# A fused two-block layer on one Trainium2 core: how the first expert layer leaves PSUM, and how its expert lists are made

## The chip, the cores and the metric

The kernel runs on one core of one Trainium2 chip. The metric is device time in microseconds (us), the median of three runs; lower is better.

## The reference

256 tokens of width 2048 pass through a first block (sliding-window attention beside a short convolution, then a gate) and a second block (a linear recurrence beside attention over selected keys, then a layer of many small experts). The change lies in that last layer, which in the reference reads:

```python
q = (xf @ wq).reshape(t, PEER_HEADS, PEER_QDIM)
...
top_s, pos = lax.top_k(cand_s, PEER_TOPK)
expert = jnp.take_along_axis(cand_i, pos, axis=-1).reshape(t, -1)
gate = jax.nn.softmax(top_s.astype(jnp.float32), axis=-1).astype(x.dtype).reshape(t, -1)
...
z = jnp.einsum('cd,ced->ce', xc, u[ec])
act = jax.nn.gelu(z, approximate=False) * gc
return jnp.einsum('ce,ced->cd', act, v[ec])
```

There are 128 x 128 = 16384 experts; each token takes 16 of them for each of 8 heads, so 128 in all.

## The kernel before

All products with weights run through one stream of weight tiles, 128 x 2048 float32 of 1 MB each (`stream`, L387). A tile is loaded into one of three `raw` buffers by SP, cut in two halves of 1024 columns, and each half is split into a high part `whi` by ACT (L415, five buffers) and a low part `wlo` by DVE (L422, four buffers), three halves ahead of the half that PE is at. One turn of the loop at L437 is one half: `cut_hi` for the half three ahead, `self.step()`, `cut_lo` for that half, the matmuls of this half, and after the last half of a pair of tiles whatever leaves PSUM. The instructions of each engine run in the order in which this loop writes them, so an instruction that waits holds all that stand behind it on its engine.

`step()` (L346) hands out the side work: it goes over the first three tasks in a list and lets each run to its next `yield`; the numbers yielded are charged against a credit for each half (1.3 in this layer, overdrafts carried over), and 0 costs nothing but a turn.

The expert layer (`peer`, L1237) streams, in this order:

- 16 tiles of `w_pq` (queries of the heads), then
- 128 tiles of `peer_u`, numbered 0 to 127 here. Together they hold every expert's first vector; the hidden products of all 16384 experts are computed and stored. From tile 24 on a half is 8 matmuls of 512 columns (L467) and 8 of 256 (L468), until then three of 256 each. After each pair of tiles `post_u` (L1577) takes it out of its PSUM buffer `mm` (two buffers of a pair): ACT copies one part (L336), DVE adds the other and multiplies by the row scale (L339, L340), ACT applies Gelu and starts the store to the table `zg` in HBM (L1581, L1582);
- one tile and then 107 rows of experts gathered from `peer_v`, by lists of the experts in use.

Beside the first two, the side work finds which experts are in use:

- `head_task` (L1291) finds the top 16 of a head on DVE and then has POOL scatter the gates into the table: 16 indirect DMAs for each half of 128 tokens (`scatter`, L1356). Scatters of the same half of two heads wait for each other, as both add into the same column of the table. Heads 0 to 2 (`EARLY` = 3) scatter both halves, heads 3 to 7 the first half alone; the second halves of heads 3 to 7 follow at the end, in `gates_task` (L1371). They are 256 indirect DMAs in all.
- `mask_task` (L1417) runs once for each half of the tokens, from the tile in `U_MASK` on. It reads the half's gates back in 8 chunks of 1 MB (SP, L1426, into four `vraw` buffers) behind the half's last scatter, and DVE takes the maximum over tokens (L1444). For the second half POOL first adds one half of the chunk to the other (L1437).
- `list_task` (L1456) turns the masks into lists of experts in 37 pieces of up to three columns of a list. A piece is: POOL compares (L1503), DVE makes the 0/1 matrix `hot` (L1510), PE multiplies it (three matmuls, L1520) into a PSUM bank, ACT takes two results from the bank (L1528, L1529), DVE sums (L1535). The banks are the two of `bg1`. Piece i's products are written in one step, its ACT part in the next, its sum in the one after.
- `row_source` (L1627) loads an expert row through the lists. It is called seven tiles ahead, by `load` (L400) from `cut_lo`, and runs `step()` until the lists are there, however many steps that takes, before the stream goes on.

```python
                    if i + RAW_BUFS + ROW_BUFS < n and callable(items[i + RAW_BUFS + ROW_BUFS][0]):
                        load(i + RAW_BUFS + ROW_BUFS)
```

Of the kernel before, what the change touches and what calls it, by code (L numbers as in the profile page):

```python
# [17 lines left out]
P = 128  # L18
# [36 lines left out]
DUMMY = P * P  # L55
U_MERGE = 24
LAST = 3
U_MASK = (63, 96)
EARLY = 3
ROWS = 7  # L60
COEF = 6

# [184 lines left out]
class Build:  # L247
# [139 lines left out]
    def stream(self, items):  # L387


        n = len(items)  # L390
        raw, cut, order = {}, {}, []
        fills = {FILL_FROM + FILL_STEP * j: j for j in range(FILLS)}
        while len(order) < 2 * n:
            i = len(order) // 2
            if items[i][1].crossed:
                order += [(i, 0), (i + 1, 0), (i, 1), (i + 1, 1)]
            else:
                order += [(i, 0), (i, 1)]

        def load(i, a=0, b=2 * HALF):  # L400
            if i < n and callable(items[i][0]):
                raw[i] = items[i][0]()
                return
            if i < n:
                if a == 0:
                    raw[i] = self.strm.tile([P, 2 * HALF], F32, name="raw", tag="raw", bufs=RAW_BUFS)
                self.nc.sync.dma_start(raw[i][:, a:b], items[i][0][:, a:b])
                if i in fills and b == 2 * HALF:
                    self.fill(fills.pop(i))

        def cut_hi(k):
            if k < 2 * n:
                i, half = order[k]
                hi = self.strm.tile([P, HALF], F32R, name="whi", tag="whi", bufs=CUT_BUFS)
                self.S.activation(hi, raw[i][:, half * HALF:(half + 1) * HALF], AF.Copy)  # L415
                cut[k] = [hi, None]

        def cut_lo(k):
            if k < 2 * n:
                i, half = order[k]  # L420
                lo = self.strm.tile([P, HALF], F32R, name="wlo", tag="wlo", bufs=CUT_BUFS - 1)
                self.V.tensor_tensor(lo, raw[i][:, half * HALF:(half + 1) * HALF], cut[k][0].bitcast(F32),  # L422
                                     op=ALU.subtract)
                cut[k][1] = lo
                if half:
                    del raw[i]
                    if i + RAW_BUFS < n and not callable(items[i + RAW_BUFS][0]):
                        load(i + RAW_BUFS)
                    if i + RAW_BUFS + ROW_BUFS < n and callable(items[i + RAW_BUFS + ROW_BUFS][0]):
                        load(i + RAW_BUFS + ROW_BUFS)  # L430

        self.prologue(load)
        for k in range(AHEAD):
            cut_hi(k)
            cut_lo(k)
            self.prologue_step(k)
        for k, (i, half) in enumerate(order):  # L437
            self.pos = i
            cut_hi(k + AHEAD)
            self.step()  # L440
            cut_lo(k + AHEAD)
            hi, lo = cut.pop(k)
            items[i][1](half, hi, lo)
            if half and items[i][2]:
                items[i][2]()
# [791 lines left out]
    def peer(self):  # L1237
# [144 lines left out]
        def begin_lists():  # L1382
            t = self.actp.tile([P, 2 * KC * TOK], F32, name="lists", tag=f"act{free}")
            at = [0]

            def cut(*dims, dt=F32):
                size = int(np.prod(dims))
                v = t[:, at[0]:at[0] + size]
                at[0] += size + size % 2
                if dt is not F32:  # L1390
                    v = v.bitcast(dt)
                if len(dims) > 1:
                    ax = " ".join("abcd"[:len(dims)])
                    v = v.rearrange(f"p ({ax}) -> p {ax}", **dict(zip("abcd", dims)))
                return v

            offsets, n = CONST_AT["consts3"]
            c3 = cut(n)
            self.nc.sync.dma_start(c3, A["consts3"])
            for name, (o, w) in offsets.items():  # L1400
                self.cons[name] = c3[:, o:o + w]
            st["abs"], st["gt"] = cut(2, PIECE * P), cut(2, PIECE, P)
            st["hot"], st["prer"] = self.t([2, PIECE * P], "hot", dt=F32R), self.t([PIECE, 3, 130], "pre", dt=F32R)
            st["scratch"] = t[:, 0:at[0]]
            st["m"], st["cls"], st["pre"] = cut(2, P), cut(3, P), cut(3, 132)
            st["n"], st["mid"], st["half"], st["end"] = (cut(3) for _ in range(4))
            st["bias"], st["high"] = cut(40), cut(40)
            st["sum"], st["row"], st["rho"] = cut(NLIST), cut(NLIST), cut(NLIST)
            st["zat"], st["vat"], st["over"] = cut(NLIST, dt=U32), cut(NLIST, dt=U32), cut(2, dt=mybir.dt.int32)
            st["zg"], st["gates"], st["cd"] = cut(ROWS, 2, TOK), cut(TOK), [None, None]  # L1410
            assert at[0] <= 2 * KC * TOK
# [5 lines left out]
        def mask_task(ti):  # L1417
            while self.pos < u0 + U_MASK[ti]:
                yield 0.0
            chunks = {}  # L1420

            def load(g):
                if g < 8:
                    gt = self.t([2 * HALF], "vraw", ROW_BUFS)
                    gv = chunks[g] = gt.rearrange("p (b t) -> p b t", b=16)
                    d = self.nc.sync.dma_start(gv, table[:, 16 * g:16 * g + 16, 1, ti * P:(ti + 1) * P])  # L1426
                    for other in scatters[1 - ti] if ti == 0 else ():
                        self.tc.declare_no_dep(d.ins, other.ins, reason="gates of other tokens")
                    behind(d, scatters[ti][-1])

            for g in range(3):
                load(g)
                yield 0.0
            def half(g):
                if ti and g < 8:
                    chunk, chunks[g] = chunks[g], chunks[g][:, :, 0:P // 2]
                    G.tensor_tensor(chunks[g], chunks[g], chunk[:, :, P // 2:P], op=ALU.add)  # L1437

            half(0)
            yield 0.0  # L1440
            for g in range(8):
                load(g + 3)
                half(g + 1)
                V.tensor_reduce(st["m"][:, ti, 16 * g:16 * g + 16], chunks[g], axis=AX.X, op=ALU.max)  # L1444
                yield 1.25 if ti else 2.3
            V.tensor_scalar(st["m"][:, ti], st["m"][:, ti], 0.0, None, op0=ALU.is_gt)
            V.memset(st["m"][:, ti, P - 1:P], 0.0)
            if ti:
                d = self.nc.sync.dma_start(st["gates"], table[:, P - 1, 1])
                for k in range(2):  # L1450
                    behind(d, scatters[k][-1])
            yield 0.2
            if ti:
                yield from list_task()

        def list_task():  # L1456
# [32 lines left out]
            for c in range(3):  # L1489
# [3 lines left out]
                    V.tensor_scalar(out[:, o:o + n], self.con("starts", o, o + n), -1.0, edge[:, c:c + 1],  # L1493
                                    op0=ALU.mult, op1=ALU.add)
                o += n
            yield 1.4

            def late(i):

# [10 lines left out]
                    V.scalar_tensor_tensor(st["hot"][:, i % 2, :n * P], self.con("slots", 0, n * P), hi[:, k:k + 1],  # L1510
                                           st["abs"][:, i % 2, :n * P], op0=ALU.is_le, op1=ALU.mult)

            banks = {}

            def products_of(i):
                if i < len(pieces):
                    c, b, n = pieces[i]
                    ps = self.bg1()
                    for j in range(n):
                        T.matmul(ps[:, 130 * j:130 * j + 130], st["hot"][:, i % 2, j * P:(j + 1) * P],  # L1520
                                 st["prer"][:, j, c], start=True, stop=True)
# [2 lines left out]
            def signs(i):  # L1524
                if 0 <= i < len(pieces):
                    c, b, n = pieces[i]
                    col, pv = CLASS_AT[c] + b, banks.pop(i)
                    S.activation(st["row"][:, col:col + n], pv[:, 0:n, P], AF.Copy)  # L1528
                    S.activation(st["gt"][:, i % 2, 0:n], pv[:, 0:n, 0:P], AF.Sign, bias=self.con("past", col, col + 1))  # L1529

            def sums(i):
                if i >= 0:
                    c, b, n = pieces[i]
                    col = CLASS_AT[c] + b
                    V.tensor_reduce(st["sum"][:, col:col + n], st["gt"][:, i % 2, 0:n], axis=AX.X, op=ALU.add)  # L1535

            late(0)
            late(1)
            yield 0.0
            yield 0.0  # L1540
            hot(0)
            yield 0.0
            for i in range(len(pieces) + 2):
                late(i + 2)
                hot(i + 1)
                sums(i - 2)
                signs(i - 1)
                products_of(i)
                yield 1.25
            rho = st["rho"]  # L1550
# [25 lines left out]

        def post_u(i):  # L1577
            def f(ps):
                z = self.t([2, TOK], "z", 3)
                self.scaled(z, ps)  # L1580
                S.activation(z, z, AF.Gelu)  # L1581
                d = self.nc.scalar.dma_start(table[:, i:i + 2, 0], z)  # L1582
                for other in scatters[0] + scatters[1]:
                    self.tc.declare_no_dep(d.ins, other.ins, reason="gates stand beside the hidden products")
                stores.append(d)
            return f

        def post_last(j):

            def f(ps):  # L1590
                if j == 0:
                    st["zlast"] = self.t([2, TOK], "z", 3)
                z = st["zlast"][:, j]
                S.activation(z, ps[:, j, 1], AF.Copy)
                V.tensor_tensor(z, z, ps[:, j, 0], op=ALU.add)
# [205 lines left out]
```

## Time and profile before

| | |
|---|---|
| median of three runs | 2518.39 us (2518.31 to 2519.71) |
| the profiled execution | 2519.8 us, of which 2518.0 us are its span |
| PE busy | 2454.8 us, 97% of the span |
| DVE, ACT, POOL busy | 1793.1, 1347.5, 815.8 us |
| mean granted TensorE clock | 0.992 of full speed |
| HBM | 218 GB/s over the span |

The profile follows one execution. The span runs from its first to its last instruction, the rest of the execution's time lies around it. A busy PE is not PE at its peak, since matmuls overlap and their ends are modelled; how fast the stream goes is read from how many matmuls of one kind start in a stretch of time. A wait is put down to what ended it.

### The profile page before, as it was taken

How to read it: one execution, taken by the hardware profiler on the slowest of the kernel's cores; microseconds unless marked ns; L12 is line 12 of the kernel's file. 1: busy time of each engine (PE TensorE's matmuls, PEld its weight loads, DVE VectorE, ACT ScalarE, POOL GpSimd, SP SyncE). 2: the span in 40 equal slices, each digit the busy share in tenths (PEclk: the TensorE clock that was granted, in tenths of full speed). 3: DMA queues.
4: the chain of work that ended last, by engine and by line, in shares of the span. 5: the costliest groups of instructions: out<-in, count | busy, mean ns of one | idle time of the engine just before them, and what ended most of it. 6: DMA issues, size and time to landing. Idle time of an engine off the chain costs nothing.

```text
span 2518.0 us, 37080 instructions
## 1 busy us (share of the span) xinstructions
PE 2454.8 (97%) x14275; PEld 2151.1 (85%) x14275; DVE 1793.1 (71%) x2840; ACT 1347.5 (54%) x1887; POOL 815.8 (32%) x525
## 2 busy tenths in 40 slices
PE   9999999999999999999999999999978899999996
PEld 7888888898888888889999888878867788778885
DVE  7677777776666777776999755575567657777776
ACT  6566555554555677754345444444435445555555
POOL 0000000000000000000788877877533435555563
PEclk9999999999999999999999999999999899999999
DMA  7545565565544665555677777897884478998984
GB/s 250 186 152 176 192 208 199 193 228 184 186 165 156 206 203 188 202 186 185 168 197 196 227 209 210 230 313 210 236 254 165 155 265 316 318 320 318 319 315 159
DMA packets 180373, 550.62 MB, mean 219 GB/s; under 512 B 47649, under 2 KB 113697, under 8 KB 124130
## 3 DMA queue, kind: packets, MB, share of 16 engines
q1 hardware_dynamic: 102082, 391.18, 45.2%
q0 software_dynamic: 60832, 140.41, 19.4%
q10 hardware_dynamic: 17280, 16.65, 1.9%
q8 instruction: 112, 1.84, 0.3%
q14 instruction: 67, 0.55, 0.1%
HBM read 512.39 MB, written 35.78 MB: 218 GB/s over the span
## 4 chain that ended last, share of the span: by engine, by line
PE 79%; issue 6%; DMA 5%; DVE 4%; POOL 4%; ACT 3%; ACTq 0%; SPq 0%; POOLq 0%; DVEq 0%
PE mm L467 36%; PE mm L468 18%; PE mm L459 4%; PE mm L460 4%; PE mm L461 4%; POOL lists L1644 2%; DMA vraw<-zg 2%; DVE wlo L422 2%; PE bg L1682 1%; PE mm L1682 1%; PE mm L1683 1%; PE mm L1681 1%; PE bg L1683 1%; PE bg L1681 1%; DMA raw<-peer_u 1%
## 5 line engine op out<-in xcount | busy, mean ns | idle before, releaser
L467 PE MATMUL mm<-act,whi 128*128 128x512 f32 x4368 | 1228.7, 399 | 8.8 <-ACT whi L415 5.3
L422 DVE TENSOR_TENSOR wlo<-raw,whi 128x1024 fp32r<-128x1024 f32 x754 | 911.7, 1233 | 218.0 <-ACT whi L415 159.9
L467 PEld LDWEIGHTS mm<-act,whi 128*128 128x128 f32 x4368 | 792.6, 190 | 133.6 <-ACT whi L415 7.5
L1359 POOL DMA_INDIRECT zg<-sel,at x256 | 474.3, 1853 | 1319.0 <-DMA raw<-w_pq 1205.3
L415 ACT ACTIVATE whi<-raw 128x1024 fp32r<-128x1024 f32 x754 | 762.4, 1050 | 153.5 <-PE mm L467 39.9
L468 PEld LDWEIGHTS mm<-act,wlo 128*128 128x128 f32 x4368 | 676.1, 191 | 78.3 <-DVE wlo L422 11.9
L468 PE MATMUL mm<-act,wlo 128*128 128x256 f32 x4368 | 702.2, 284 | 8.3 <-DVE wlo L422 8.2
L459 PE MATMUL mm<-act,whi 128*128 128x256 f32 x768 | 218.1, 284 | 0.0
L461 PE MATMUL mm<-act,wlo 128*128 128x256 f32 x768 | 217.5, 283 | 0.2 <-DVE wlo L422 0.2
L460 PE MATMUL mm<-act,whi 128*128 128x256 f32 x768 | 217.3, 283 | 0.0
L336 ACT ACTIVATE z<-mm 128x512 f32<-128x512 f32 x106 | 63.2, 597 | 273.8 <-PE mm L467 273.7
L339 DVE TENSOR_TENSOR z<-z,mm 128x512 f32<-128x512 f32 x106 | 72.8, 686 | 156.5 <-ACT z L336 155.9
L422 DVE TENSOR_TENSOR wlo<-vraw,whi 128x1024 fp32r<-128x1024 f32 x124 | 148.8, 1231 | 38.5 <-ACT whi L415 31.3
L1654 ACT ACTIVATE parts<-lists 128x256 fp32r<-128x256 f32 x107 | 44.7, 418 | 193.9 <-DVE lists L1652 193.9
L461 PEld LDWEIGHTS mm<-act,wlo 128*128 128x128 f32 x768 | 146.9, 191 | 0.6 <-DVE wlo L422 0.6
L460 PEld LDWEIGHTS mm<-act,whi 128*128 128x128 f32 x768 | 147.0, 191 | 0.2
L459 PEld LDWEIGHTS mm<-act,whi 128*128 128x128 f32 x768 | 147.0, 191 | 0.0
L1682 PE MATMUL bg<-wlo,parts 128*128 128x512 f32 x316 | 127.5, 403 | 4.0 <-DVE wlo L422 4.0
L1644 POOL DMA_INDIRECT lists<-zg,lists x107 | 116.8, 1092 | 33.2 <-issue 32.0
L1682 PE MATMUL mm<-wlo,parts 128*128 128x512 f32 x316 | 123.9, 392 | 3.4 <-DVE wlo L422 3.4
L1681 PE MATMUL bg<-whi,parts 128*128 128x512 f32 x316 | 123.9, 392 | 1.9 <-ACT whi L415 1.8
L415 ACT ACTIVATE whi<-vraw 128x1024 fp32r<-128x1024 f32 x124 | 125.0, 1044 | 0.1
(337 smaller groups left out, 2624.0 us busy)
## 6 DMA issues: line engine op xcount, KB each, us to landing
raw<-peer_u SPq DMA_DIRECT2D x128, 1024.0 KB, 5.4
raw<-w_in SPq DMA_DIRECT2D x50, 1024.0 KB, 4.9
raw<-w_rnn SPq DMA_DIRECT2D x48, 1024.0 KB, 5.0
zg<-zero SPq DMA_DIRECT2D x16, 1024.0 KB, 8.7
raw<-w_out SPq DMA_DIRECT2D x16, 1024.0 KB, 4.9
raw<-w_ple_gate SPq DMA_DIRECT2D x16, 1024.0 KB, 5.6
raw<-w_q SPq DMA_DIRECT2D x16, 1024.0 KB, 4.9
raw<-w_o SPq DMA_DIRECT2D x16, 1024.0 KB, 5.2
```

What stands on the lines that cost most here:

```text
L339: self.V.tensor_tensor(out, out, ps[:, :, 0], op=ALU.add)
L415: self.S.activation(hi, raw[i][:, half * HALF:(half + 1) * HALF], AF.Copy)
L422: self.V.tensor_tensor(lo, raw[i][:, half * HALF:(half + 1) * HALF], cut[k][0].bitcast(F32), op=ALU.subtract)
L459: self.T.matmul(ps, wh, ah, start=first, stop=False)
L460: self.T.matmul(ps, wh, al, start=False, stop=False)
L461: self.T.matmul(ps, wl, ah, start=False, stop=last)
L467: high = lambda i: self.T.matmul(ps, hi[:, ws[i]], both[i], start=(first and i == 0), stop=(last and i == n - 1))
L468: low = lambda i: self.T.matmul(ps[:, 0], lo[:, ws[i]], both[i][:, 0], start=False, stop=False)
L1359: d = G.indirect_dma_start(cells, bass.IndirectOffsetOnAxis(st["at"][:, ti, k:k + 1], 0), st["sel"][:, 2, ti, k:k + 1], None, bounds_check ...
L1644: d = G.indirect_dma_start(st["zg"][:, v % ROWS].rearrange("p n t -> p (n t)"), None, rows, bass.IndirectOffsetOnAxis(st["zat"][:, b:b + 1 ...
L1681: T.matmul(ps, ch[:, ts], hi, start=False, stop=False)
L1682: T.matmul(ps, ch[:, ts], lo, start=False, stop=False)
```

## The change

1. `post_u` no longer empties a pair at once. It puts `hidden_task` at the front of the side work: a turn that does nothing, then in three further steps the copy; the addition and the multiplication; Gelu and the store. There are four `z` buffers in place of three. The last pairs (from tile 124 on) still leave at once.
2. The products of the list pieces go in turn to the two banks of `bg1` and to the two of `bg2`, which lay idle in this layer, and ACT takes a piece up two steps after its products, not one; `gt` has three buffers.
3. `mask_task` yields once more in each chunk, ahead of the maximum. It starts at tiles 79 and 90, not 63 and 96.
4. `EARLY` is 6: heads 0 to 5 scatter both halves, one after the other, and only the second halves of heads 6 and 7 are left for the end.
5. A row of experts is no longer loaded when its turn comes but queued until the lists are there, or until it is wanted four tiles ahead.

```diff
-U_MASK = (63, 96)
-EARLY = 3
+U_MASK = (79, 90)
+EARLY = 6
...
-                        load(i + RAW_BUFS + ROW_BUFS)
+                        rows.append(i + RAW_BUFS + ROW_BUFS)
+                    while rows and ("lists" in self.flags or rows[0] <= i + ROW_BUFS):
+                        load(rows.pop(0))
...
                 half(g + 1)
+                yield 0.0
                 V.tensor_reduce(st["m"][:, ti, 16 * g:16 * g + 16], chunks[g], axis=AX.X, op=ALU.max)
...
-            banks = {}
+            banks, more = {}, self.bg2()
...
-                    ps = self.bg1()
+                    ps = self.bg1() if i % 4 < 2 else more[:, i % 4 - 2]
...
-            for i in range(len(pieces) + 2):
+            for i in range(len(pieces) + 3):
                 late(i + 2)
                 hot(i + 1)
-                sums(i - 2)
-                signs(i - 1)
+                sums(i - 3)
+                signs(i - 2)
                 products_of(i)
...
         def post_u(i):
             def f(ps):
-                z = self.t([2, TOK], "z", 3)
-                self.scaled(z, ps)
-                S.activation(z, z, AF.Gelu)
-                d = self.nc.scalar.dma_start(table[:, i:i + 2, 0], z)
...
+                if i < P - 4:
+                    self.spawn(hidden_task(i, ps), front=True)
+                else:
+                    for _ in hidden_task(i, ps):
+                        pass
             return f
+
+        def hidden_task(i, ps):
+
+            yield 0.0
+            z = self.t([2, TOK], "z", 4)
+            merged = len(ps.shape) == 4
+            if merged:
+                S.activation(z, ps[:, :, 1], AF.Copy)
+                yield 0.0
+                V.tensor_tensor(z, z, ps[:, :, 0], op=ALU.add)
+            V.tensor_tensor(z, z if merged else ps, self.bc2(self.row), op=ALU.mult)
+            yield 0.0
+            S.activation(z, z, AF.Gelu)
+            d = self.nc.scalar.dma_start(table[:, i:i + 2, 0], z)
```

How this moves instructions stands at two places. The first is ACT while the list pieces run (`whi` is the high part of a weight half, `z` a pair that leaves PSUM, `bg` a bank of list products, `lists` the side work's store). Before:

```order
L415 ACTIVATE whi<-raw 128x1024
L1528 ACTIVATE lists<-bg_18446 128x3
L1529 ACTIVATE lists<-bg_18446,lists 128x384
L336 ACTIVATE z<-mm 128x512
L1581 ACTIVATE z<-z 128x512
L1582 DMA zg<-z 128x2x256
L415 ACTIVATE whi<-raw 128x1024
L1528 ACTIVATE lists<-bg_18477 128x3
L1529 ACTIVATE lists<-bg_18477,lists 128x384
```

Changed:

```order
L415 ACTIVATE whi<-raw 128x1024
L1593 ACTIVATE z<-mm 128x512
L1530 ACTIVATE lists<-bg_18269 128x3
L1531 ACTIVATE lists<-bg_18269,lists 128x384
L415 ACTIVATE whi<-raw 128x1024
L1530 ACTIVATE lists<-bg_18298 128x3
L1531 ACTIVATE lists<-bg_18298,lists 128x384
L415 ACTIVATE whi<-raw 128x1024
L1598 ACTIVATE z<-z 128x512
L1599 DMA zg<-z 128x2x256
L1530 ACTIVATE lists<-bg_17847 128x3
L1531 ACTIVATE lists<-bg_17847,lists 128x384
```

The copy and Gelu stood side by side, with DVE's addition and multiplication between them in time; two halves of other work of ACT stand between them now, and bank 17847 is the pair `bg2`.

The second is DVE at the masks of the second half of the tokens (`wlo` is the low part of a weight half, `vraw` a chunk of the table). Before:

```order
L1444 TENSOR_REDUCE lists<-vraw 128x16
L422 TENSOR_TENSOR wlo<-raw,whi 128x1024
L1444 TENSOR_REDUCE lists<-vraw 128x16
L422 TENSOR_TENSOR wlo<-raw,whi 128x1024
L339 TENSOR_TENSOR z<-z,mm 128x512
L340 TENSOR_TENSOR z<-z,rstd 128x512
L1444 TENSOR_REDUCE lists<-vraw 128x16
L422 TENSOR_TENSOR wlo<-raw,whi 128x1024
L1444 TENSOR_REDUCE lists<-vraw 128x16
```

Changed:

```order
L1447 TENSOR_REDUCE lists<-vraw 128x16
L422 TENSOR_TENSOR wlo<-raw,whi 128x1024 x2
L1447 TENSOR_REDUCE lists<-vraw 128x16
L422 TENSOR_TENSOR wlo<-raw,whi 128x1024
L1595 TENSOR_TENSOR z<-z,mm 128x512
L1596 TENSOR_TENSOR z<-z,rstd 128x512
L422 TENSOR_TENSOR wlo<-raw,whi 128x1024
L1447 TENSOR_REDUCE lists<-vraw 128x16
```

A maximum stood behind every half of a tile; one stands behind every second half now, that is one for each tile. At the masks of the first half, too, there is one for each tile in the changed order, where there were eight in six and a half tiles.

## Rows read from the trace of the kernel before

**Rows 1.** Windows, L467 alone: width, PE (x started), PEld (x), clock, DMA share, GB/s.
```profile
1400.00:1640.00 240.00, 186.25 (x686) 123.17 (x684) 1.00 0.79 222
1640.00:1690.00 50.00, 35.56 (x128) 23.00 (x128) 1.00 1.04 318
...
1830.00:1875.00 45.00, 22.84 (x72) 14.86 (x72) 0.89 0.87 266
1875.00:1994.00 119.00, 79.16 (x259) 47.55 (x258) 0.96 0.47 162
1994.00:2012.00 18.00, 6.95 (x21) 4.70 (x22) 0.72 0.37 126
```

**Rows 2.** Groups of instructions, 1600 to 1700 us: busy, mean ns, idle before them.
```profile
L1444 DVE TENSOR_REDUCE lists<-vraw 128x16 f32<-128x2048 f32 x8 | 18.2, 2278 | 4.1 <-DMA vraw<-zg 4.1
```

**Rows 3.** The same view, 1830 to 1875 us.
```profile
L1444 DVE TENSOR_REDUCE lists<-vraw 128x16 f32<-128x1024 f32 x6 | 7.3, 1216 | 13.1 <-POOL vraw L1437 13.1
```

**Rows 4.** Waits of PE, 1830 to 1875 us: in total, times, longest.
```profile
PE mm L468 <- DVE wlo L422: 7.0, 4, 3.4
PE bg L1468 <- DVE lists L1464: 5.0, 1, 5.0
```

**Rows 5.** Waits of PE, 1875 to 1994 us.
```profile
PE bg L1520 <- ACT lists L1529: 11.7, 7, 1.7
```

**Rows 6.** Timeline of all engines, 1936 to 1948 us: start, us, engine and line.
```profile
1936.56 1.60 PE L467 MATMUL mm<-act,whi 128*128 128x512 f32 x6
1936.62 1.25 POOL L1503 TENSOR_SCALAR lists<-lists 128x384 f32<-128x384 f32 x1 [1.04 <-DVE hot L1510]
1936.91 1.37 DVE L422 TENSOR_TENSOR wlo<-raw,whi 128x1024 fp32r<-128x1024 f32 x1
...
1939.72 1.59 PE L467 MATMUL mm<-act,whi 128*128 128x512 f32 x6
...
1942.78 0.60 ACT L336 ACTIVATE z<-mm 128x512 f32<-128x512 f32 x1 [4.71 <-PE mm L467]
...
1944.85 0.63 ACT L1581 ACTIVATE z<-z 128x512 f32<-128x512 f32 x1 [1.48 <-DVE z L340]
...
1946.96 0.57 ACT L1529 ACTIVATE lists<-bg,lists 128x384 f32<-128x384 f32 x1
...
1947.58 0.55 PE L1520 MATMUL bg<-pre,hot 128*128 128x130 f32 x3 [1.70 <-ACT lists L1529]
```

**Rows 7.** Groups of instructions of DVE, 1860 to 2010 us.
```profile
L422 DVE TENSOR_TENSOR wlo<-raw,whi 128x1024 fp32r<-128x1024 f32 x40 | 50.8, 1278 | 18.5 <-ACT whi L415 12.3 <-issue 3.7 <-PE mm L468 2.5
...
L1510 DVE SCALAR_TENSOR_TENSOR hot<-lists 128x384 fp32r<-128x384 f32 x34 | 22.0, 646 | 0.6 <-POOL lists L1503 0.6
...
L1535 DVE TENSOR_REDUCE lists<-lists 128x3 f32<-128x384 f32 x34 | 18.4, 544 | 0.2 <-ACT lists L1529 0.2
...
L340 DVE TENSOR_TENSOR z<-z,rstd 128x512 f32<-128x512 f32 x10 | 6.9, 692 | 0.3
```

**Rows 8.** Timeline of POOL: the 1st, 112th, 193rd and last of the 256 scatters.
```profile
1206.52 1.91 POOL L1359 DMA_INDIRECT zg<-sel,at  x1 [1205.26 <-DMA raw<-w_pq]
...
1447.03 1.64 POOL L1359 DMA_INDIRECT zg<-sel,at  x1 [0.30 <-issue]
...
1645.95 1.55 POOL L1359 DMA_INDIRECT zg<-sel,at  x1 [6.09 <-DMA zg<-sel,at]
...
1792.16 2.42 POOL L1359 DMA_INDIRECT zg<-sel,at  x1 [0.30 <-issue]
```

**Rows 9.** Timeline of SP, the first chunk of each half; and landing of all L1426.
```profile
1619.15 1.39 SPq L1426 DMA_DIRECT2D vraw<-zg  x1
...
1805.90 0.43 SPq L1426 DMA_DIRECT2D vraw<-zg  x1
...
DMA to landing us min/median/max: 8.7/10.7/13.4
```

**Rows 10.** DMA issues of the page: KB each, median us to landing.
```profile
raw<-peer_u SPq DMA_DIRECT2D x128, 1024.0 KB, 5.4
```

More of the change, by code (lines that the diff above doesn't have):

```diff
@@ L390, in stream @@
         n = len(items)
-        raw, cut, order = {}, {}, []
+        raw, cut, order, rows = {}, {}, [], []
         fills = {FILL_FROM + FILL_STEP * j: j for j in range(FILLS)}
@@ L1401, in begin_lists @@
                 self.cons[name] = c3[:, o:o + w]
-            st["abs"], st["gt"] = cut(2, PIECE * P), cut(2, PIECE, P)
+            st["abs"], st["gt"] = cut(2, PIECE * P), cut(3, PIECE, P)
             st["hot"], st["prer"] = self.t([2, PIECE * P], "hot", dt=F32R), self.t([PIECE, 3, 130], "pre", dt=F32R)
@@ L1495, in list_task @@
                 o += n
-            yield 1.4
             def late(i):
@@ L1528, in signs @@
                     S.activation(st["row"][:, col:col + n], pv[:, 0:n, P], AF.Copy)
-                    S.activation(st["gt"][:, i % 2, 0:n], pv[:, 0:n, 0:P], AF.Sign, bias=self.con("past", col, col + 1))
+                    S.activation(st["gt"][:, i % 3, 0:n], pv[:, 0:n, 0:P], AF.Sign, bias=self.con("past", col, col + 1))
             def sums(i):
@@ L1534, in sums @@
                     col = CLASS_AT[c] + b
-                    V.tensor_reduce(st["sum"][:, col:col + n], st["gt"][:, i % 2, 0:n], axis=AX.X, op=ALU.add)
+                    V.tensor_reduce(st["sum"][:, col:col + n], st["gt"][:, i % 3, 0:n], axis=AX.X, op=ALU.add)
             late(0)
+            yield 1.4
             late(1)
-            yield 0.0
-            yield 0.0
             hot(0)
-            yield 0.0
-            for i in range(len(pieces) + 2):
+            yield 0.6
+            for i in range(len(pieces) + 3):
                 late(i + 2)
                 hot(i + 1)
-                sums(i - 2)
-                signs(i - 1)
+                sums(i - 3)
+                signs(i - 2)
                 products_of(i)
@@ L1578, in f @@
             def f(ps):
-                z = self.t([2, TOK], "z", 3)
-                self.scaled(z, ps)
-                S.activation(z, z, AF.Gelu)
-                d = self.nc.scalar.dma_start(table[:, i:i + 2, 0], z)
-                for other in scatters[0] + scatters[1]:
-                    self.tc.declare_no_dep(d.ins, other.ins, reason="gates stand beside the hidden products")
-                stores.append(d)
-            return f
+                if i < P - 4:
[3 more added lines that the diff above has]
+                        pass
+            return f
+        def hidden_task(i, ps):
[10 more added lines that the diff above has]
+            d = self.nc.scalar.dma_start(table[:, i:i + 2, 0], z)
+            for other in scatters[0] + scatters[1]:
+                self.tc.declare_no_dep(d.ins, other.ins, reason="gates stand beside the hidden products")
+            stores.append(d)
+            yield 0.0
         def post_last(j):
@@ L1591, in f @@
                 if j == 0:
-                    st["zlast"] = self.t([2, TOK], "z", 3)
+                    st["zlast"] = self.t([2, TOK], "z", 4)
                 z = st["zlast"][:, j]
```

## The prediction

> **What bounds the kernel now.** I read the shares first: PE is busy for 97% of the span, so nothing is won by making another engine faster where PE keeps its pace. Then I asked where it does not keep it, with the windows of L467 alone [rows 1]. In the first window 686 matmuls start in 240 us, 0.350 us each; a half of a tile has 8 of them, so a half takes 2.80 us and a tile 5.60. That is the stream at its own pace. In every other window the time lost is its width less 0.350 us for each L467:
>
> - 1640 to 1690, masks of the first half of the tokens: 50 - 128 x 0.35 = 5.2 us
> - 1830 to 1875, masks of the second half and the start of the lists: 45 - 72 x 0.35 = 19.8
> - 1875 to 1994, list pieces: 119 - 259 x 0.35 = 28.4
> - 1994 to 2012, the last pieces, run without the stream: 18 - 21 x 0.35 = 10.7
>
> This is 64.1 us. What follows asks of each stretch what ends its waits and whether the change removes it. Elsewhere the stream is at pace, so emptying pairs in steps is worth nothing there.
>
> **List pieces.** Two halves that each carry one piece start at 1936.56 and 1939.72 [rows 6], 3.16 us apart and not 2.80: a piece costs PE 0.35 us of its own, and 37 of them 13.0 us. That stays. The rest is a wait that PE meets in seven places, 11.7 us in all, always for ACT's sign [rows 5], and the half clock that follows some of them (granted 0.96 of full speed in this window, 0.72 in the next, [rows 1]). One instance is in the timeline [rows 6]: ACT's copy of a pair can start only when PE has ended it, at 1942.78; Gelu then waits for DVE until 1944.85; the next high part and the sign stand behind Gelu, so the sign starts at 1946.96 and PE, which needs that bank, at 1947.58, 1.70 us late. The change takes both links away. Copy, addition and Gelu stand in different halves, each issued when what it needs is done, and with four banks the sign of a piece is due four halves after its products, not two. What could bind next is DVE: in a half 1.28 for the low part, 0.65 for hot, 0.54 for the sum, and a quarter of two operations of 0.69 for a pair, together 2.82 us [rows 7] against 3.15 of PE. It fits with 10% to spare. I take 1 us beside the 13.0. From below the rest is 0; from above it is 13 us, if DVE came to 3.5 us a half (37 x 0.35).
>
> **The last pieces.** The first row load stands at tile 121 before, and it runs the side work until the lists are there; the last pieces then go by without a tile between them, 10.7 us. In the changed order the lists end ahead of tile 123, and the queue forces nothing before tile 124. So the 10.7 us go; the pieces themselves are already counted. The first rows are loaded some four tiles, 22 us, before their split, against 10.7 us that a chunk of the same size needs to land [rows 9]. If the lists came later than tile 124, the steps would be forced again: 0 is the lower end, 10.7 the upper.
>
> **Masks of the second half.** PE waits 7.0 us for low parts and 5.0 for DVE at the start of the lists [rows 4]; DVE was held by POOL's additions for 13.1 us [rows 3], which wait for chunks. A chunk needs 8.7 to 13.4 us to land [rows 9] and was used three halves, 8.4 us, after its issue. With one chunk for each tile it has three tiles, 16.8 us. Two costs take the place of this wait. The first is the start. SP reached the first chunk at 1805.90, behind the load of tile 99 [rows 9]; it now stands behind that of tile 93, so six tiles, 33.6 us, earlier, and 3 us earlier again if the first masks lose 2 us instead of 5.2: 1769. It must wait for the last scatter. The 112 scatters up to 1447.03 alternate and start 2.17 us apart [rows 8]. From there on the same half mostly follows itself, and the first scatter of a head waits for the landing of the head before, as at 1645.95, for 6.09 us; of eight such waits (2.9 to 6.1 us, 38 in all) the changed order keeps two. The last scatter, which started at 1792.16, would end at about 1206.5 + 255 x 2.17 + 2 x 5 + 2 = 1771, and land some 6 us later. So SP waits about 7 us, with the load of tile 94 and all later ones behind it. Three `raw` buffers are 16.8 us of lead, less 5.4 for a load to land [rows 10] and 2.6 for the two low parts: some 8 us, into which the wait just fits. The second cost is bandwidth. Load, chunk and store are 2.23 MB for a tile; at the 318 GB/s of the masks of the first half [rows 1] this takes 7.0 us, not 5.6, over eight tiles 11 us, against some 8 us of lead. I take 4 us for this stretch: 0 if all is covered, 18 (11 and 7) if nothing is.
>
> **Masks of the first half.** Eight maxima of 2.28 us [rows 2] and their chunks now fall on eight tiles, not six and a half. DVE needs 2 x 1.28 + 0.69 + 2.28 = 5.53 us for a tile of 5.60 [rows 2, 7], and no longer stands behind ACT's copy of a pair. The first chunk moves from behind tile 66, 1619.15 [rows 9], to behind tile 82: 16 x 5.60 later, 1709. It now waits for scatter 224, not 176: 1206.5 + 223 x 2.17 + 5 + 2 = 1697, landing at 1703. That is 6 us in hand. Bandwidth is as above, with the scatters beside it. I take 2 us; the ends are 0 and 11.
>
> **The rest.** The pair's PSUM buffer is read three halves later; it is wanted again five halves after its end, which covers it with 5.6 us, except where DVE is already late. The steps at the front of the side work cost no credit, and the changed order shows heads and masks at their places. The rows' phase after 2050 us is the same work. Each counts 0.
>
> **The sum.** Left are 2 + 4 + 13 + 1 = 20 us of 64.1; 44.1 are saved. The profiled execution took 2519.8 us in all, so 2475.7; it lay 1.4 above the median, so **2474.3 us**.
>
> **A rule against it.** POOL's comparison at 1936.62 and DVE's low part at 1936.91 overlap for 0.96 us, and the low part took 1.37 [rows 6] where the mean of the stretch is 1.28 [rows 7]: 0.09 us more, not 0.96. The Trainium skill, SBUF — State Buffer, section Who interferes with whom, says that a VectorE instruction with two SBUF inputs and a GpSimd instruction that reads SBUF shut each other out entirely, the later waiting for the earlier to end. By that rule the denser pieces would let each comparison hold DVE for its whole length; the row shows a tenth of it, so I count the row.
>
> **The rivals.**
>
> - *Everything is covered.* The masks lose nothing: 51.1 us saved, 2467. For it: the lead of 8 to 10 us against a backlog of 7 to 11. Chance 0.17.
> - *The masks stay as costly.* If bandwidth is the true limit there (share above 1.0 in the first masks [rows 1]), the 25.0 us of both stay but for their spread; with only the pieces and the drain won, 39.1 - 14 = 25 us are saved, 2493. Chance 0.11.
> - *POOL and DVE exclude each other.* A half needs 2.82 + 1.25 = 4.07 us of DVE and not 3.15, 37 x 0.92 = 34 us more than forecast: 2508. It is the rule above; against it stands the overlap. Chance 0.04.
> - *SP is held by the scatters, and it is slower than before.* This has one place: the first chunk of the first masks stands ahead of the load of tile 83 on SP and now waits for scatter 224. Each us beyond some 8 us of lead after 1709 is lost on PE. With 44 us saved elsewhere it decides when scatter 224 lands after 1709 + 8 + 44 = 1761, 58 us later than worked out. Were all scatters as slow as the last (2.42 + 0.30), it would land at about 1206.5 + 223 x 2.72 + 13 = 1826, and the time would be 2474 + 109 = 2583. Against it: the alternating 112 took 2.17. Chance 0.03.
> - *It does not do what it says*: lists that end too late keep the drain, 10.7 us, 2485. The order speaks against it. Chance 0.03.
>
> **How the numbers follow.** The forecast has the remaining 0.62. A measurement of this kernel can tell 0.2%, 5 us, from no change. The range runs from 2465, two below full cover, to 2495, which takes in costly masks, or a DVE that runs over its 10%; outside are the exclusion of POOL and DVE, the held SP, and a little of either side. Faster holds for every case but the held SP and what I have not thought of: 0.94. The same 0.03, slower 0.03.
>
> **What would show it.** Right: L467 starts at 0.35 us each through the masks, a piece costs 0.35 us and no wait of PE for ACT's sign is left; pieces end with the stream running; POOL's scatters show two waits and end near 1770. Wrong: SP held at the first chunk beyond 8 us; DVE over 3.15 us a half among the pieces; low parts that wait for `raw` loads in both masks.

## The result and the profile after

| | before | after |
|---|---|---|
| median | 2518.39 us (2516.76 to 2519.98, 5 runs) | 2531.13 us (2529.42 to 2533.20, 5 runs) |
| ratio to before | | 1.0051, 95% interval 1.0040 to 1.0062 |
| span of the profiled execution | 2518.0 us | 2529.3 us |
| mean granted clock | 0.992 | 0.986 |

The change makes the kernel 12.7 us slower; the forecast was 2474.3 us, 44 us faster. The windows of the high products' line in the changed kernel (L469, which was L467) stand against [rows 1]:

```profile
1400.00:1640.00 240.00, 186.16 (x687) 123.32 (x686) 1.00 0.77 213
...
1700.00:1765.00 65.00, 23.07 (x85) 14.91 (x83) 0.75 0.36 54
1765.00:1840.00 75.00, 48.71 (x167) 31.56 (x167) 0.90 1.05 310
...
1885.00:2008.00 123.00, 93.35 (x317) 56.44 (x315) 1.00 0.61 203
```

The list pieces are as forecast: 123 us less 317 x 0.35 leaves 12.0 us, against 28.4 before. But from 1700 to 1765 us only 85 products start where 186 would fit, the DMA engines move 54 GB/s, and the granted clock falls to 0.75, and 0.90 in the window behind it. What PE waits for from 1700 to 1800 us, and what SP waits for from 1690 to 1800 us (line waited for: total, times, longest):

```profile
PE mm L469 <- ACT whi L415: 40.1, 1, 40.1
PE mm L469 <- DVE z L1595: 6.0, 1, 6.0
```

```profile
SPq L1428 <- DMA zg<-sel,at: 56.5, 1, 56.5
SPq L407 <- DVE wlo L422: 34.3, 8, 5.2
```

SP's timeline shows where. Its first chunk of the first masks (L1428) stands ahead of a weight load, and SP arrives there at 1691.88 + 11.53 = 1703.4:

```profile
1691.88 11.53 SPq L407 DMA_DIRECT2D raw<-peer_u  x3
1759.95 0.38 SPq L1428 DMA_DIRECT2D vraw<-zg  x1
1760.42 2.04 SPq L407 DMA_DIRECT2D raw<-peer_u  x1
```

So SP stood 56.5 us for scatter 224 with all weight loads behind it. The scatters are late: from 1447 to 1640 us (the stretch ahead of the masks) there are 81 in the kernel before and 69 in the changed one (line, engine, operation, count, busy us, mean ns; then POOL's idle time before them and what ended it):

```profile
L1359 POOL DMA_INDIRECT zg<-sel,at x81 | 151.9, 1876 | 41.2 <-issue 24.0 <-DVE z L340 11.4 <-DMA zg<-sel,at 5.8
```

```profile
L1361 POOL DMA_INDIRECT zg<-sel,at x69 | 172.2, 2495 | 21.0 <-issue 21.0
```

The changed kernel's POOL does wait less between scatters (only the 0.30 us of an issue, no landing of another head), as the alternation meant, but each takes 2.495 us instead of 1.876. From no. 97 to about no. 203 they start 2.80 us apart, which is the length of a half. No. 224 starts at 1756.8, and started at 1713.8 before.

The time behind the pace, taken at the start of a half as its time less that of tile 24 and less 2.80 us for each half between, shows where each kernel lost (the rest of the work, from the last L469 to PE's end, is in the last row). The last column is an experiment told below:

| us lost | before | forecast left | after | low parts split |
|---|---|---|---|---|
| tiles 24 to 99 (first masks) | 5.9 | 2 | 57.5 | 0.8 |
| tiles 99 to 104 (second masks, lists start) | 20.1 | 4 | 3.1 | 3.6 |
| tiles 104 to 123.5 (pieces, drain) | 39.3 | 14 | 11.6 | 11.6 |
| last tiles | 1.6 | | 1.6 | 1.6 |
| last L467 to PE's end | 457.6 | as before | 462.7 | 460.8 |

All of the miss lies in the first row but for the 5 us of the last, which lies between 457 and 464 us among kernels that do not touch it; why it varies stays unexplained.

### The profile page after: what moved, and what is told of

The parts are those of the page before. It is cut to its first block, busy times and chain, and to the rows that moved or that the text cites. A ratio compares the mean times of both kernels' runs of the same rounds, so it can differ in the third digit from the quotient of the medians.

```text
span 2529.3 us, 37132 instructions
## 1 busy us (share of the span) xinstructions
PE 2445.1 (97%) x14275; PEld 2148.0 (85%) x14275; DVE 1788.4 (71%) x2840; ACT 1352.6 (53%) x1887; POOL 874.7 (35%) x525
## 5 line engine op out<-in xcount | busy, mean ns | idle before, releaser
L469 PE MATMUL mm<-act,whi 128*128 128x512 f32 x4368 | 1227.8, 398 | 57.2 <-ACT whi L415 41.9
L415 ACT ACTIVATE whi<-raw 128x1024 fp32r<-128x1024 f32 x754 | 778.6, 1053 | 494.5 <-PE mm L469 261.6
L1361 POOL DMA_INDIRECT zg<-sel,at x256 | 534.3, 2087 | 1292.7 <-DMA raw<-w_pq 1205.7
L469 PEld LDWEIGHTS mm<-act,whi 128*128 128x128 f32 x4368 | 791.3, 189 | 181.2 <-ACT whi L415 42.8
L1698 PE MATMUL mm<-whi,parts 128*128 128x512 f32 x316 | 124.2, 393 | 3.2 <-PEq L1718 3.0
L1700 PE MATMUL mm<-whi,parts 128*128 128x512 f32 x316 | 124.2, 393 | 0.0
```

What stands on the lines that cost most here:

```text
L469: high = lambda i: self.T.matmul(ps, hi[:, ws[i]], both[i], start=(first and i == 0), stop=(last and i == n - 1))
L1361: d = G.indirect_dma_start(cells, bass.IndirectOffsetOnAxis(st["at"][:, ti, k:k + 1], 0), st["sel"][:, 2, ti, k:k + 1], None, bounds_check ...
L1698: T.matmul(ps, ch[:, ts], hi, start=False, stop=False)
L1700: T.matmul(ps, cl[:, ts], hi, start=False, stop=last)
```

## The experiments

All ratios are to the kernel before, with 95% intervals.

**Theory A**: when pairs leave in spread steps, DVE's low parts come exactly one each half, and the scatters on POOL lock to them, one for each half. **Rival B**: halves that alternate scatter more slowly (two columns of the table, no landing between). First the one part undone, and done alone.

```diff
-                if i < P - 4:
+                if False:
```

> The changed kernel, with every pair emptied at once again (copy, addition, multiplication, Gelu and store behind the pair's last half); four banks, mask chunks one per tile, alternating scatters and the start tiles 79 and 90 stay. Theory A, that the even spacing of DVE's low parts holds POOL's scatters to one per half: scatters from the 97th on return from 2.80 us a piece to about 2.2, scatter 224 starts near 1700 and not at 1757, SP's wait at the first chunk falls from 56 us to under 10, and the time to about 2480 (2470 to 2495). Rival B, that two halves of the tokens in flight at once make the scatters themselves slow: they stay at 2.80, SP waits over 50 us, the time stays near 2531.

Measured: 2503.69 us, ratio 0.9938 (0.9921 to 0.9955). With alternating halves kept, scatters are 2.0 to 2.3 us apart, no. 224 starts at 1695.4 and the last at 1769.6; SP waits for none. B falls. The time is above the expected range (2470 to 2495): the pieces lose 33.7 us, with four banks, and PE waits for signs again (1875 to 2000 us):

```profile
PE bg L1522 <- ACT lists L1531: 13.7, 8, 1.8
```

The other way round, the kernel before with `hidden_task` and the four `z` buffers only:

> The kernel before, with nothing of the change but the three spread steps in which a pair leaves PSUM (and the fourth z buffer); scatters in the old order, masks at tiles 63 and 96. Theory A: scatters from the 97th on start 2.80 us apart at best, the last of the first half starts near 1645 to 1665 and not at 1604, the last of all near 1870 to 1890 and not at 1792; SP waits some 30 us at the first masks and some 50 at the second, and the time is 2550 to 2590. Rival B: scatters keep their 2.2 us and their eight waits, SP hardly waits, and the time is 2490 to 2515.

Measured: 2536.1 us, ratio 1.0069 (1.0052 to 1.0086). The direction was right, the size too large: the scatters of one half slowed to 2.75 to 3.08 us from no. 97 on but not from no. 161 to 208 (2.2 to 2.4), and SP waited in both masks:

```profile
SPq L1426 <- DMA zg<-sel,at: 51.3, 2, 27.3
```

So the steps alone, with halves that do not alternate, bring the slow scatters. They also remove the pieces' sign waits with two banks (9 us lost there beside the drain's 11).

Next, two kernels that break the even cadence in different ways. The low part in two instructions, in the whole program:

```diff
-                self.V.tensor_tensor(lo, raw[i][:, half * HALF:(half + 1) * HALF], cut[k][0].bitcast(F32),
-                                     op=ALU.subtract)
+                for a in (0, HALF // 2):
+                    cs = slice(a, a + HALF // 2)
+                    self.V.tensor_tensor(lo[:, cs], raw[i][:, half * HALF:(half + 1) * HALF][:, cs],
+                                         cut[k][0].bitcast(F32)[:, cs], op=ALU.subtract)
```

> The changed kernel, with each low part of 1024 columns made by two DVE instructions of 512 columns. Theory A, with the holder named as the single low-part instruction that a scatter meets at its start: the scatter waits for half as long, so its step falls from 2.80 us to 2.4 or less, SP's wait at the first chunk from 56 us to under 20, and the time to about 2490 (2475 to 2510). If a scatter is slow for another reason (two halves in flight, or the pace of the DMA queue), the step stays at 2.80 and the time near 2531.

Measured: 2492.54 us, ratio 0.9897 (0.9881 to 0.9914). Scatters are 1.87 us apart from no. 97 on, no. 224 starts at 1655.9, SP waits for none, and only 19.5 us are lost up to tile 127. But the rows' phase (the expert rows, from the last high product to PE's end) takes 476.8 us and not 460: there DVE computes two low parts of 0.686 us for one of 1.222.

```diff
-                if i < P - 4:
+                if 90 <= i < P - 4:
```

> The changed kernel, with pairs emptied at once up to tile 88 and in spread steps from tile 90 on, when most scatters are out. Theory A: scatters at about 2.2 us until 1750, SP's wait at the first chunk under 10 us, list pieces at 0.35 us each with no wait for ACT's sign; about 2478 (2468 to 2492), which beats both kernels. Rival B: 2.80 us a scatter, and near 2531.

Measured: 2480.75 us, ratio 0.9853 (0.9836 to 0.9869). Pairs leave at once until tile 90, when the scatters are over; scatters are as in the first experiment (no. 224 at 1696.0), and the pieces lose 11.6 us.

Then the split only where scatters run beside the stream (tiles 0 to 77), with all pairs in steps:

```diff
+                n_lo = 2 if self.base and 0 <= i - self.base - 16 < 78 else 1
+                for a in range(0, HALF, HALF // n_lo):
+                    cs = slice(a, a + HALF // n_lo)
...
```

> The changed kernel with every pair leaving in steps, but the low parts of tiles 0 to 77 of the first expert vectors are computed in two DVE instructions of 512 columns; all other low parts of the program are one instruction again. If the locking of scatters to one per half is broken by the shorter instruction alone, and the 16 us that the run with all low parts split lost behind 2002 us belong to its split low parts there: scatter 224 starts near 1656, no wait of SP at the first chunk, the last L467 near 2002, the rows' phase 460 us and not 477, so about 2477 us in all. If the long rows' phase comes from something else (the scatters that end early, or the clock), it stays 477 us and the time near 2492. If splitting must hold longer than tile 77, scatters behind it go back to 2.80 us: 256 starts some 15 us later, near 1740, which the masks at tile 90 (1769) still allow.

Measured: 2474.39 us, ratio 0.9830 (0.9813 to 0.9846): faster than both kernels. The rows' phase takes 460.8 us, so the 16 us were its split low parts. Scatters from 1447 to 1640 us, and the windows of the high products (L472 here):

```profile
L1364 POOL DMA_INDIRECT zg<-sel,at x103 | 161.5, 1568 | 33.6 <-issue 30.2 <-DMA zg<-sel,at 2.8 <-DVE wlo L425 0.6
```

```profile
1400.00:1640.00 240.00, 186.24 (x687) 123.52 (x686) 1.00 0.87 214
...
1700.00:1814.00 114.00, 88.33 (x327) 58.47 (x325) 1.00 1.03 325
1814.00:1849.00 35.00, 25.05 (x89) 15.87 (x89) 1.00 0.87 300
1849.00:1961.00 112.00, 85.33 (x287) 51.46 (x287) 1.00 0.59 191
```

The first masks, at 325 GB/s, lose nothing (327 x 0.35 = 114.5).

What the other parts are worth, each on the kernel with late steps. Two banks and the shorter lag, as before the change:

```diff
-                    ps = self.bg1() if i % 4 < 2 else more[:, i % 4 - 2]
+                    ps = self.bg1()
...
-                sums(i - 3)
-                signs(i - 2)
+                sums(i - 2)
+                signs(i - 1)
```

> Pairs leave in steps from tile 90 on, and the four banks and the longer lag of ACT are undone: products go to the two banks of bg1, ACT takes a piece up one step later, as before the change. If the steps alone remove PE's waits for signs (as the run with the steps alone indicated), a half with a piece stays at 3.15 us and the time is that of four banks within 3 us: 2478 to 2484. If four banks are needed too, the waits of about 2.3 us in every fourth half come back: some 33 us less what the shorter pieces hide, 2500 to 2515.

Measured: 2479.03 us, ratio 0.9845 (0.9828 to 0.9861). The pieces lose 11.5 us, and PE has no wait for a sign. Four banks are worth nothing beside the steps.

```diff
-EARLY = 6
+EARLY = 3
```

> Pairs leave in steps from tile 90 on, and EARLY is 3 as before the change, so five heads scatter the second half at the end, each scatter waiting for the head before. If the alternation of halves is worth what the forecast said (8 waits of 2.9 to 6.1 us against 2), scatter 176 is early (about 1605) and the first masks wait for nothing, while the last scatter starts near 1792 to 1800 against the chunk of tile 90 at about 1772: SP waits 25 to 35 us there, some 8 of it covered: 2495 to 2510 us. If the alternation is worth nothing, the last scatter starts near 1770 as with EARLY = 6, and the time is 2481.

Measured: 2492.61 us, ratio 0.9908 (0.9879 to 0.9937). The last scatter starts at 1785.4, and SP waits at the second masks; the wait was overestimated, the alternation is still worth some 12 us (5 to 18, as the four runs lie between 2485.6 and 2499.3):

```profile
SPq L1428 <- DMA zg<-sel,at: 11.8, 1, 11.8
```

> Pairs leave in steps from tile 90 on, and the low parts of tiles 0 to 77 are split in two DVE instructions. If the only cost left of the scatters beside the stream is their end at 1769 beside the masks, they now end near 1725 and the masks lose some 4 us less: 2474 to 2478. If the split itself costs DVE time that delays the pairs that leave at once in that stretch, it loses up to 4 us against the run with late steps: 2481 to 2485.

Measured (both edits together): 2483.56 us, ratio 0.9869 (0.9853 to 0.9886). The scatters end at 1723.5, but nothing is gained: where pairs still leave at once, through tile 89, and at their change to steps, 9.4 us are lost by tile 99, where the split with steps throughout loses 0.8. Tile 24, too, starts 2.4 us later than with late steps alone (1402.7 against 1400.3). Here the split pays only with steps throughout.

The last two test a rule that the traces gave (it is told in the last section): a scatter that starts while DVE runs an instruction with both inputs in SBUF takes until that ends and 1.42 us more. The first is the split until tile 77, cut at another column:

```diff
-                n_lo = 2 if self.base and 0 <= i - self.base - 16 < 78 else 1
-                for a in range(0, HALF, HALF // n_lo):
-                    cs = slice(a, a + HALF // n_lo)
+                two = self.base and 0 <= i - self.base - 16 < 78
+                for cs in (slice(0, 768), slice(768, HALF)) if two else (slice(0, HALF),):
...
```

> As the run with low parts split until tile 77, but into 768 and 256 columns. The rule read from the traces is that a scatter which starts while a DVE instruction runs takes until that instruction's end and 1.42 us more, and the next scatter starts 0.30 us later. A lock of one scatter for each half then needs a DVE instruction longer than 2.80 - 1.42 - 0.30 = 1.08 us. 768 columns lie between 0.69 us (512) and 1.23 us (1024), about 0.96 us: by the rule no lock, scatters 1.9 to 2.2 us apart from no. 97 on, no. 224 between 1656 and 1700, no wait of SP at the first chunk of masks, 2472 to 2480 us in all. If instead the whole low part (both pieces, some 1.3 us) shuts the scatter out, or one that is merely close to evenly spaced locks, the step stays 2.6 to 2.80 us, SP waits, and the time is 2515 to 2531.

Measured: 2475.01 us, ratio 0.9823 (0.9807 to 0.9839), scatters 1.87 us apart, no. 224 at 1658.5. The piece of 768 columns takes 0.96 us, less than the 1.08 worked out, and does not lock them: the rule's side of the two.

The last is the kernel before with the split of 512 columns until tile 77 and nothing else:

> The kernel before the change, with the low parts of tiles 0 to 77 in two DVE instructions of 512 columns and nothing else changed. By the rule the scatters of the first halves no longer wait for 1.23 us instructions: steps about 1.9 us but for the landings between heads, the last scatter near 1745 and not 1792. SP never waited for the scatters before, so this should give little: at most the 5.2 us that the first masks lost beside the scatters, 2512 to 2519 us. If DVE loses by the extra instructions where pairs leave at once, it is slower, 2519 to 2525.

Measured: 2522.87 us, ratio 1.0014 (1.0004 to 1.0024). The last scatter starts at 1748.6 and not at 1792.2, but the last L467 starts at 2048.6 against 2048.8: earlier scatters bring nothing where SP does not wait for them. By the interval the kernel is 1 to 6 us slower, in the range of the second expectation. DVE's extra instructions explain it only in part: tile 24 starts 3.0 us later (1402.6 against 1399.6), but both masks together lose some 3 us less, and the profiled run's 3 us more lie in the rows' phase.

## Why the prediction was wrong

**The step that failed** is the pace of the scatters, and with it the time of scatter 224, for which the first masks wait. The prediction took "the alternating 112 took 2.17" for all 256, and set scatter 224 at 1697, "landing at 1703", with "6 us in hand" at the first masks. The 2.17 us were measured where pairs leave at once; the changed kernel's first 96 scatters still came 2.08 to 2.36 us apart, beside the heads' work on DVE, and from no. 97 on, in tile 27, 2.80. Where only the steps were undone, no. 224 started at 1695.4 and the last at 1769.6, against 1697 and 1771 worked out (1703.1 and 1773.2 with late steps and two banks): the arithmetic was right, for a kernel without the early steps.

**What stands behind it** is a cost that was set at nothing: "Elsewhere the stream is at pace, so emptying pairs in steps is worth nothing there", and "The rest … Each counts 0". For PE this holds. But DVE's waits were POOL's room. From 1447 to 1640 us, DVE waited before and now for:

```profile
DVE z L339 <- ACT z L336: 38.2, 16, 2.4
DVE wlo L422 <- ACT whi L415: 37.6, 17, 2.2
```

```profile
DVE wlo L422 <- PE mm L470: 86.1, 69, 1.6
```

Before, DVE stood for each pair, then ran up to three low parts together, and waited again; scatters that started in its waits took 1.55 us. Now every low part waits for PE alone, so they come one each half and never leave a scatter alone: all 69 scatters of this stretch start in a low part, where 31 of the 81 did before.

**The rival that came true** was the held SP, given 0.03, with the place, the wait and the point of decision as they came: by its sum a landing at 1761 would eat the 44 us saved. SP was released at 1759.95; having arrived at 1703.4, not 1709, it lost 49.9 us at tiles 82 to 85 rather than 44: PE's 40.1 us of standing and, right behind it, a 6.0 us wait for a pair to leave PSUM and a clock granted at half in part. Its price for slow scatters, 2.72 us for all, was too high because only some 107 of the 256 slowed. The chance was wrong, for the reason above: no row of scatters beside evenly spaced low parts existed before, and the range of their cost was not bounded by the longer scatters that the trace did show (2.42 us, used for that rival alone).

**Point by point.** *List pieces*: right, 11.6 us lost against 14 forecast with the start; but the credit to four banks was wrong, since two banks with steps do the same and four banks without steps lose 33.7. *Last pieces*: right; the drain is gone in every kernel that has the queued rows, and 11 us of it stayed in the steps alone. *Second masks*: right, 3.1 us against 4. *First masks*: the bandwidth part was right or too high (0.8 us with split low parts against 2). *POOL and DVE exclude each other*: among the pieces it cost nothing, as forecast (pieces at 0.35 us). But the row set against the rule [rows 6] shows one order only, POOL's comparison first. A comparison that starts in a low part is held (changed kernel, POOL and DVE, 1902 to 1903 us):

```profile
1901.97 1.74 POOL L1505 TENSOR_SCALAR lists<-lists 128x384 f32<-128x384 f32 x1
```

```profile
1901.38 1.22 DVE L422 TENSOR_TENSOR wlo<-raw,whi 128x1024 fp32r<-128x1024 f32 x1
```

It ends 1.11 us after the low part. In all twelve kernels 49 of 408 comparisons of this size start in a low part; they take 1.54 to 3.74 us, and none ends sooner than 1.11 us after it. Of the other 359, all but two take 1.24 to 1.27 us. It cost PE nothing, and so it was set aside; a hold of the same kind made the scatters late. Both end as long behind the low part as they take alone, less 0.13 us (1.11 of 1.24, 1.42 of 1.55).

With the lock broken, the kernel takes 2474.39 us, the forecast's 2474.3. That the two agree to 0.1 us is partly luck: by the table the stream saved some 5 us more than forecast, and the rows' phase took some 3 us longer than before.

## What to carry to other kernels

When a change evens out one engine's work, look at who used the gaps: list the instructions on neighbouring engines whose duration varies in the trace (1.55 to 2.5 us here), and find what runs when a long one starts before taking their mean for the new order. A mean pace from one stage should not be carried into another with a different rhythm. Where two instructions collide and their times together fill a period (2.95 us in one of 2.80 here), a shorter first piece (768 of 1024 columns) can release the other; and in-order queues with loads behind a wait turn a small slowing far away into a stop.

## What the hardware showed that was not expected

POOL's and DVE's timelines in the changed kernel, 1656 to 1666 us (start, us, engine, line, idle before and what ended it):

```profile
1657.18 2.50 POOL L1361 DMA_INDIRECT zg<-sel,at  x1 [0.30 <-issue]
1659.99 2.47 POOL L1361 DMA_INDIRECT zg<-sel,at  x1 [0.30 <-issue]
```

```profile
1657.03 1.23 DVE L422 TENSOR_TENSOR wlo<-raw,whi 128x1024 fp32r<-128x1024 f32 x1 [1.59 <-PE mm L470]
1659.81 1.23 DVE L422 TENSOR_TENSOR wlo<-raw,whi 128x1024 fp32r<-128x1024 f32 x1 [1.56 <-PE mm L470]
```

The scatter starts 0.15 us after the low part, whose end is at 1658.26, and takes 1.42 us from there, to 1659.68. The next starts 0.30 later, again just behind the next low part's start. 1.23 + 1.42 + 0.30 = 2.95 us is longer than a half, so it never gets ahead: one scatter for each half. In the kernel before:

```profile
1547.83 1.64 POOL L1359 DMA_INDIRECT zg<-sel,at  x1 [0.30 <-issue]
1549.78 1.55 POOL L1359 DMA_INDIRECT zg<-sel,at  x1 [0.30 <-issue]
1551.63 2.42 POOL L1359 DMA_INDIRECT zg<-sel,at  x1 [0.31 <-issue]
...
1636.45 1.55 POOL L1359 DMA_INDIRECT zg<-sel,at  x1 [0.30 <-issue]
```

```profile
1547.36 0.69 DVE L340 TENSOR_TENSOR z<-z,rstd 128x512 f32<-128x512 f32 x1
1550.26 3.50 DVE L422 TENSOR_TENSOR wlo<-raw,whi 128x1024 fp32r<-128x1024 f32 x3 [2.21 <-ACT whi L415]
...
1636.39 2.29 DVE L1444 TENSOR_REDUCE lists<-vraw 128x16 f32<-128x2048 f32 x1 [2.03 <-DMA vraw<-zg]
```

The scatter at 1547.83 starts in a multiplication that ends at 1548.05 and takes 1.42 us more. The one at 1549.78 starts with DVE idle and takes 1.55, though a low part begins 0.48 us later, and that one is not longer either. The one at 1636.45 starts in a maximum of 2.29 us, with one SBUF input, and takes 1.55 as if nothing ran; so do the seven, over all kernels, that start in an addition from PSUM (L339 before) with 0.17 to 0.65 us of it left. With "the longer of 1.55 us and the time to the end of the running low part or multiplication plus 1.42 us", the durations of all but 12 of 1063 scatters between 1447 and 1640 us, in all twelve kernels, come out within 0.03 us. The 12 left started within 0.05 us of the start of a low part and took 1.55; there the low part took longer, 1.30 us instead of 1.22 in the one of full size, and 0.72 to 0.74 instead of 0.69 in the split ones.

The Trainium skill, SBUF — State Buffer, section Who interferes with whom, says that a VectorE instruction with two SBUF inputs contends with a GpSimd instruction that reads SBUF, and that a reduction never does; the traces agree, with 2.50 against 1.55 us, with the comparisons held among the pieces and with the 1.55 us beside the maximum. The same section infers that such a two-input instruction does not stall the DMAs whose descriptors GpSimd writes. For these indirect DMAs the measurement says otherwise, but only for what runs when the DMA instruction starts. That the scatter reads its list of rows from SBUF just then would fit; no run here shows what it reads when.
